# Weight parts by turns in one tile: a projection kernel whose stationary reads step by 8 bytes

## The chip, the cores and the metric

The kernel runs on one core of one Trainium2 chip. The metric is the device time of one execution in microseconds. The time of the kernel before is the median of three runs; a profiled execution of the same program is read beside them.

## What is computed

One decoder layer on x of 512 tokens by 1024 channels, in float32. The input is RMS-normalised, projected by `w_in`, passed through four token mixers, gated, merged and projected once more:

```python
h = rmsnorm(x, norm_pre)
u = h @ w_in                                   # 1024 x D_IN, D_IN holds all projections
branches = (gdn(u), gla(u), ssd(u), nsa(u))    # four mixers of 512 channels each
gates = sigmoid(u['merge_gate'])               # 4 x 1024 channels
merged = sum(gates[n] * (branches[n] @ w_br[n]) for n in range(4))
x = x + rmsnorm(merged @ w_out, norm_post)
```

Most of the arithmetic is `h @ w_in`: 84 blocks of 1024 by 128 (or 512 by 256) weights.

## The kernel before, in words

Matrix products are done in float32r, a float32 type that TensorE takes in one pass and in which it keeps fewer bits. So that no precision is lost, each operand is split into a high part (rounded to float32r) and a low part (what the rounding left), and each product is three matmuls: high by high, high by low and low by high (`mm3`, L759). The normalised input is held all the time in `hhi` and `hlo`, tiles of 128 partitions by 8 blocks by 512 tokens (L678, L679).

A block of weights is fetched by SyncE's queue into a staging tile `ws`, 128 by 1024 float32. ScalarE copies it to `wh` (the high part), VectorE subtracts that from `ws` and writes `wl` (the low part). This is `wload` (L735 to L757). `ws` has three buffers, `wh` and `wl` two each (L611). The first two loads have their low part made by GpSimd (L752).

Three kinds of products use these weights:

- `proj_ft` (L765) gives 128 channels by 512 tokens. Weights are the stationary operand: 8 slices of 128 columns of `wh` and of `wl`, loaded 24 times for 24 matmuls of 512 columns over `hhi` and `hlo`. Such a matmul is written `big<-hhi,wh` in the profile: output, moving operand, stationary operand. The first two calls run in halves of 256 columns and in another order.
- `proj_tf` and the output projection (L781) give 128 tokens by 256 channels. There the weights are the moving operand, in slices of 256 columns, and `hhi` or `hlo` is the stationary one (`tf<-wh,hhi`).
- The branch projections in `merge` (L1689) use weights from `w_br` as the stationary operand, with the split branch output `yh`, `yl` moving (`big<-yh,wh`).

One more group, at L808 to L822, puts 56 narrow columns into a `wh` tile and multiplies with 120 and 56 stationary columns.

The order of instructions is not the order of the code. `Sched` (L303) records every operation with the buffers it touches, prices it, and places all of them by a list scheduler on a model of the five engines; `emit` (L477) then issues them in that order. Dependencies in that plan come from `View.mask` (L131), which marks a tile in groups of 8 elements. Tags in `S.fifo` (L613) are handed out in the order of the load groups. Tiles without a tag live in one pool and get their address when they are first issued; those in `S.first` (L682) come ahead of all others. The waits on the chip are worked out from the operations as issued.

In all traces every instruction carries line L519, that of the helper which records it; so groups are told apart by tile names.

Of the kernel before, what the change touches and what calls it, by code (L numbers as in the profile page):

```python
# [7 lines left out]
F32 = mybir.dt.float32  # L8
BF16 = mybir.dt.bfloat16
F32R = mybir.dt.float32r  # L10
# [5 lines left out]
P = 128  # L16
# [3 lines left out]
ND = D // P  # L20
# [17 lines left out]
def f32(ap):  # L38
    return ap.bitcast(F32)


NG = 34
N4 = 12
# [555 lines left out]
def block_kernel(ctx, tc, a, out):  # L599
    nc = tc.nc  # L600
    W = a['w_in'][0]
# [6 lines left out]
    psum = mkpool("psum", space=PSUM)  # L608
    dram = mkpool("dram", space=bass.MemoryType.DRAM)
    pools = {None: (const, 1), 'big': (psum, 3), 'sm': (psum, 5)}  # L610
    for tag, n in (('g', NG), ('t4', N4), ('ws', 3), ('wh', 2), ('wl', 2), ('cv', 3), ('k1', 10), ('tiny', 12)):  # L611
        pools[tag] = (work, n)
    S = Sched(tc, pools, ('ws', 'wh', 'wl', 'cv', 'big'))  # L613
    act, dve, pool, pe, sp = (Engine(S, e, r) for e, r in (('ACT', nc.scalar), ('DVE', nc.vector), ('POOL', nc.gpsimd),
                                                            ('PE', nc.tensor), ('SP', nc.sync)))
    after = S.order

    def big(name="big"):
        return S.buf(name, [P, T], F32, 'big', 'psum')

    def sm(name="sm"):
        return S.buf(name, [P, T], F32, 'sm', 'psum')

    def w2(name, cap=None, dt=F32):
        return S.buf(name, [P, T], dt, 'g')

# [3 lines left out]
    def t4(name, dt=F32, shape=(P, 2, T)):  # L630
        return S.buf(name, shape, dt, 't4')

# [12 lines left out]
    def cst(name, shape, dt=F32):  # L645
        return S.buf(name, shape, dt, None)
# [30 lines left out]
    loads = []  # L677
    hhi = cst("hhi", [P, ND, T], F32R)  # L678
    hlo = cst("hlo", [P, ND, T], F32R)  # L679

    al12 = cst("al12", [P, 12], F32)
    S.first += [al12, hhi, hlo]  # L682
    xts = []
    for tt in range(NT):
        xt = t4("xt", shape=(P, D))
# [38 lines left out]
    pe.transpose(pt[:, :P], rows, ident)  # L724
    act.copy(cols, pt[:, :P])

    dtb12 = cst("dtb12", [P, 12], F32)
    for dst, na, ncc in ((al12, 'a_log_a', 'a_log_c'), (dtb12, 'dt_bias_a', 'dt_bias_c')):
        for nm, o, n in ((na, 0, 4), (ncc, 4, 8)):
            src = a[nm]  # L730
# [1 line left out]
    dskip = bcast_row('d_skip_c', 8)  # L732


    def wload(srcs, cut, shape, res=(), group=True):  # L735

        if group:
            S.grp += 1
        st, hi, lo = (S.buf(nm, [P, 1024], dt, nm).rearrange(cut, **shape)
                      for nm, dt in (('ws', F32), ('wh', F32R), ('wl', F32R)))  # L740
        o = 0
        for i, src in enumerate(srcs):
            n = src.shape[-1]
            op = sp.dma_start(st[:, :, o:o + n], src)
            if i == 0:
                op.resv = [v.buf for v in res]
            loads.append(op)
            o += n
        early = len(loads) <= 2
        S.urgent = 0 if early else -1  # L750
        c = act.copy(hi, st)
        t = (pool if early else dve).tensor_sub(lo, st, f32(hi))  # L752
        S.urgent = None
        if early:

            c.key, t.key = (0, xload.prio[1] + 40), (0, xload.prio[1] + 41)
        return hi, lo, op  # L757

    def mm3(ps, sh, sl, mh, ml, first, last, shared=False):  # L759
        i = pe.matmul(ps, sh, mh, start=first, stop=False, skip_group_check=shared)  # L760
        pe.matmul(ps, sh, ml, start=False, stop=False, skip_group_check=shared)
        pe.matmul(ps, sl, mh, start=False, stop=last, skip_group_check=shared)
        return i

    def proj_ft(c0, *res, group=True):  # L765
        hi, lo, _ = wload([W[:, c0:c0 + P].rearrange("(a p) f -> p a f", p=P)], "p (a f) -> p a f", dict(f=P), res, group)
        ps = big()
        if len(loads) > 2:
            for d in range(ND):
                mm3(ps, hi[:, d], lo[:, d], hhi[:, d], hlo[:, d], d == 0, d == ND - 1)  # L770
            return ps

        for o in (0, T // 2):
            t = slice(o, o + T // 2)
            pairs = [(hi, hhi, d) for d in range(ND)] + [(hi, hlo, d) for d in range(ND)] + [(lo, hhi, d) for d in range(ND)]
            for i, (w, m, d) in enumerate(pairs):
                pe.matmul(ps[:, t], w[:, d], m[:, d, t], start=i == 0 and o == 0, stop=i == len(pairs) - 1,
                          skip_group_check=True)
        return ps
# [15 lines left out]
    def tf_load(srcs, kh, res=(), group=False):  # L795
        hi, lo, _ = wload([src[kh * 512:(kh + 1) * 512].rearrange("(a p) f -> p a f", p=P) for src in srcs],
                          "p (a f) -> p a f", dict(f=256), res, group)
        return hi, lo
# [9 lines left out]
    S.grp += 1  # L808
    late = []
    LO = 64  # L810
    st, hi = (S.buf(nm, [P, 1024], dt, nm).rearrange("p (a f) -> p a f", f=P) for nm, dt in (('ws', F32), ('wh', F32R)))
    for nm, o, n in (('gla_gk', 0, 16), ('gdn_beta', 16, 8), ('ssd_dt', 24, 8), ('nsa_gate', 32, 24)):
        src = W[:, OFF[nm]:OFF[nm] + n].rearrange("(a p) f -> p a f", p=P)
        late.append(sp.dma_start(st[:, :, o:o + n], src))
# [114 lines left out]
    def zproj_ft(name):  # L929
        z = Feat("z")  # L930
        for c in range(4):
            ps = proj_ft(OFF[name] + c * P, z[c])
            silu2(z[c], ps)
        return z
# [54 lines left out]
    def gdn():  # L989
        qkv = [None] * 12  # L990
        for c in (4, 5, 6, 7, 0, 1, 2, 3, 8, 9, 10, 11):
            if c < GPAIR:
                if c % 2 == 0:
                    pair = t4("gqk")
                t = pair[:, c % 2]
            else:
                t = w2("gqkv")
            ps = proj_ft(OFF['gdn_q'] + c * P, t)
            conv_silu(t, ps, R_CA, 12, c, None)
            qkv[c] = t  # L1000
            n = sum(v is not None for v in qkv)
            if n <= 2:
                loads[-1].key = (0, xload.prio[1] + 0.1 * n)
            elif n == 4:
                for i, op in enumerate(late):
                    op.key = (1, len(S.ops) - 1 + 0.1 * (i + 1))
# [199 lines left out]
    def ssd():  # L1206
        xbc = []
        for c in range(8):
            t = w2("gqkv")
            ps = proj_ft(OFF['ssd_x'] + c * P, t)  # L1210
            conv_silu(t, ps, R_CC, 8, c, cols[:, R_CB + c:R_CB + c + 1])
            xbc.append(t)
# [476 lines left out]
    def merge(n):  # L1689
# [5 lines left out]
        for d2 in range(ND // 2):  # L1695
            ds = (2 * d2, 2 * d2 + 1)
            first = merged[ds[0]] is None
            if first:
                for d in ds:
                    merged[d] = w2("merged")  # L1700
            ths = []
            for i, d in enumerate(ds):
                psg = proj_ft(OFF['merge_gate'] + n * D + d * P, *([merged[v] for v in ds] if first and i == 0 else []),
                              group=i == 0)
                if i == 0:
                    for e in ready:
                        S.order(loads[-1], e)
                th = S.buf("mth", [P, T], F32, 'cv')
                act.activation(th, psg, AF.Tanh, scale=0.5)
                ths.append(th)  # L1710
            src = a['w_br'][0, n][:, d2 * 256:(d2 + 1) * 256].rearrange("(b p) f -> p b f", p=P)
            hi, lo, _ = wload([src], "p (b f) -> p b f", dict(f=256), group=False)
            for i, d in enumerate(ds):
                th = ths[i]
                ps = big()
                for b in range(4):
                    fs = slice(i * P, (i + 1) * P)
                    mm3(ps, hi[:, b, fs], lo[:, b, fs], yh[b], yl[b], b == 0, b == 3)
                if first:
                    dve.scalar_tensor_tensor(merged[d], th, 1.0, ps, op0=OP.add, op1=OP.mult)  # L1720
                else:
                    dve.scalar_tensor_tensor(th, th, 1.0, ps, op0=OP.add, op1=OP.mult)
                    m_ops.append(pool.tensor_add(merged[d], merged[d], th))
# [17 lines left out]
    for q in range(4):  # L1741
# [9 lines left out]
        else:  # L1751
# [3 lines left out]
            for tt in range(NT):  # L1755
                for d in range(ND):
                    s = slice(tt * P, (tt + 1) * P)
                    hi, lo = parts[d // 4]
# [49 lines left out]
```

## Time and profile before

| | us |
|---|---|
| median of 3 runs | 824.61 (823.39 to 826.69) |
| profiled execution, its own time | 824.95 |
| span in the profile, first to last instruction | 823.2 |
| TensorE matmul busy | 798.4 (97%) |
| TensorE weight loads busy | 678.2 (82%) |
| VectorE busy | 500.3 (61%) |
| ScalarE busy | 373.8 (45%) |
| GpSimd busy | 206.6 (25%) |

The busy time of matmuls overlaps itself, since one starts before the one ahead of it has drained: the length of a matmul in a row says less than the distance from its start to the start of the next. Weight loads are recorded apart (PEld); the load for a matmul runs beside the matmul ahead of it. The mean granted TensorE clock is 0.995 of full speed.

### The profile page before, as it was taken

To read this page: it belongs to the slowest core of one execution; us is meant where nothing else is said; L and a number is where in the kernel's file an instruction comes from. 1 tells how busy PE (TensorE), PEld (TensorE's weight loads), DVE (VectorE), ACT (ScalarE), POOL (GpSimd) and SP (SyncE) were. 2 spreads that over 40 slices of the span, in tenths; PEclk is the share of its full clock that TensorE was granted. 3 is DMA by queue.
4 is the path that set the end of the run, shared out by engine and by line. 5 is a ranking of instruction groups with operands and counts; after the bars stand their busy time and mean duration, and the time that the engine had idled before them with its cause. 6 is when DMAs were issued, how large, how long until landed. Compare 5 with 4: busy or idle time off the path is not lost.

```text
span 823.2 us, 12822 instructions
## 1 busy us (share of the span) xinstructions
PE 798.4 (97%) x4772; PEld 678.2 (82%) x4772; DVE 500.3 (61%) x1112; ACT 373.8 (45%) x878; POOL 206.6 (25%) x254
## 2 busy tenths in 40 slices
PE   5999999999999999999999899998999999999996
PEld 5888888887888899888887677897888888888996
DVE  5687766577545767777775977748533333343535
ACT  5344734323335767677654734644432222223432
POOL 6000273340131322222213400205521411121101
PEclk9999999999999999999999999999999999999998
DMA  7434254510132122211223231433133333334332
GB/s 229 93 105 128 77 136 105 129 27 2 52 103 76 52 53 52 77 52 53 68 61 77 52 77 52 115 104 103 52 97 85 101 102 103 87 94 127 115 143 103
DMA packets 112742, 72.39 MB, mean 88 GB/s; under 512 B 11788, under 2 KB 108232, under 8 KB 112680
## 3 DMA queue, kind: packets, MB, share of 16 engines
q1 hardware_dynamic: 111976, 69.86, 30.6%
q0 software_dynamic: 704, 1.70, 0.9%
q8 instruction: 38, 0.62, 0.3%
q14 instruction: 24, 0.20, 0.1%
HBM read 68.12 MB, written 3.43 MB: 87 GB/s over the span
## 4 chain that ended last, share of the span: by engine, by line
PE 89%; DVE 4%; ACT 2%; issue 2%; POOL 1%; DMA 1%; POOLq 0%; SPq 0%; DVEq 0%; ACTq 0%
PE big L519 58%; PE tf L519 12%; PE p_nsa L519 9%; PE p_gdn L519 5%; PE p_gla L519 2%; PE p_ssd L519 2%; DMA xt<-in_x 1%; DVE wl L519 1%; PE p_head_tail L519 1%; DVE gb L519 0%; POOL se L519 0%; ACT sq L519 0%; ACT wh L519 0%; PE p_h L519 0%; DVE cv L519 0%
## 5 line engine op out<-in xcount | busy, mean ns | idle before, releaser
L519 DVE TENSOR_TENSOR wl<-ws,wh 128x1024 fp32r<-128x1024 f32 x108 | 149.3, 1382 | 157.5 <-ACT wh L519 156.2
L519 PE MATMUL big<-hhi,wh 128*128 128x512 f32 (+2 forms) x632 | 242.4, 391 | 0.0
L519 PE MATMUL big<-hlo,wh 128*128 128x512 f32 (+1 forms) x632 | 241.3, 389 | 0.0
L519 PE MATMUL big<-hhi,wl 128*128 128x512 f32 (+1 forms) x624 | 237.3, 388 | 0.0
L519 ACT CAST wh<-ws 128x1024 fp32r<-128x1024 f32 (+1 forms) x111 | 116.1, 1047 | 243.0 <-PE big L519 199.3
L519 PEld LDWEIGHTS big<-hhi,wh 128*128 128x128 f32 (+1 forms) x632 | 118.1, 191 | 22.7 <-issue 0.5
L519 PEld LDWEIGHTS big<-hlo,wh 128*128 128x128 f32 x632 | 116.7, 188 | 22.8 <-issue 0.6
L519 PEld LDWEIGHTS big<-hhi,wl 128*128 128x128 f32 x624 | 115.7, 189 | 22.0 <-issue 0.8
L519 PE MATMUL tf<-wl,hhi 128*128 128x256 f32 x288 | 81.9, 285 | 0.0
L519 PE MATMUL tf<-wh,hhi 128*128 128x256 f32 x288 | 81.9, 285 | 0.0
L519 PE MATMUL tf<-wh,hlo 128*128 128x256 f32 x288 | 81.8, 285 | 0.0
L519 POOL TENSOR_SCALAR se<-se,r,ngate 128x128 f32<-128x128 f32 (+1 forms) x64 | 41.4, 649 | 152.8 <-DVE r L519 120.6
L519 POOL TENSOR_TENSOR merged<-merged,mth 128x512 f32<-128x512 f32 x24 | 33.1, 1379 | 143.8 <-DVE mth L519 143.8
L519 PEld LDWEIGHTS tf<-wh,hhi 128*128 128x128 f32 x288 | 55.0, 191 | 0.5
L519 PEld LDWEIGHTS tf<-wl,hhi 128*128 128x128 f32 x288 | 55.1, 192 | 0.4
L519 PEld LDWEIGHTS tf<-wh,hlo 128*128 128x128 f32 x288 | 55.1, 191 | 0.4
L519 PE MATMUL big<-yl,wh 128*128 128x512 f32 x128 | 50.3, 393 | 0.0
L519 PE MATMUL big<-yh,wh 128*128 128x512 f32 x128 | 50.1, 392 | 0.0
L519 PE MATMUL big<-yh,wl 128*128 128x512 f32 x128 | 50.1, 392 | 0.0
L519 ACT ACTIVATE se<-se,mn 128x128 f32<-128x128 f32 (+1 forms) x64 | 36.0, 563 | 24.1 <-DVE mn L519 22.8
L519 DVE SCALAR_TENSOR_TENSOR cv<-big,cols,cv 128x511 f32<-128x511 f32 (+2 forms) x60 | 44.5, 743 | 1.4 <-ACT cv L519 0.5
L519 DVE CUSTOM_DVE_ANT_0 se<-p_nsa,nb 128x128 f32<-128x128 f32 (+1 forms) x64 | 30.9, 482 | 8.1 <-PE p_nsa L519 7.7
(335 smaller groups left out, 1241.7 us busy)
## 6 DMA issues: line engine op xcount, KB each, us to landing
ws<-in_w_in SPq DMA_DIRECT2D x84, 512.0 KB, 3.9
ws<-in_w_br SPq DMA_DIRECT2D x16, 512.0 KB, 3.5
ws<-in_w_out SPq DMA_DIRECT2D x8, 512.0 KB, 3.4
rows<-scrG SPq DMA_DIRECT2D x12, 256.0 KB, 4.7
xt<-in_x SPq DMA_DIRECT2D x4, 512.0 KB, 3.5
xr<-in_x SPq DMA_DIRECT2D x4, 512.0 KB, 4.5
out<-xo SPq DMA_DIRECT2D x8, 256.0 KB, 2.6
scrA<-B POOLq DMA_DIRECT2D x4, 256.0 KB, 3.1
```

Of the source, the lines that this page charges most:

```text
L519: return fn(*[res(v) for v in args], **{k: res(v) for k, v in kw.items()})
```

## The change

`wh` and `wl` become one tile of 2048 float32r and 32 more that nothing uses (8320 bytes for each partition), with two buffers under one tag `w`. Since 8320 is 32 times 256 and 128 more, the second buffer begins at another remainder modulo 256 than the first. A new helper `wtile` gives the two halves. With `turns` the high and low part of each weight stand next to each other, so that a slice of 128 columns of either part spans 1024 bytes in steps of 8; without it the high parts fill the first 4096 bytes and the low parts the next. Only `proj_ft` asks for `turns`, and only from its third load on. The branch projections, the token-major projections and the narrow group use the tile without it. `dtb12`, 48 bytes, is allocated right behind `hlo` instead of later.

```diff
-    for tag, n in (('g', NG), ('t4', N4), ('ws', 3), ('wh', 2), ('wl', 2), ('cv', 3), ('k1', 10), ('tiny', 12)):
+    for tag, n in (('g', NG), ('t4', N4), ('ws', 3), ('w', 2), ('cv', 3), ('k1', 10), ('tiny', 12)):
...
-    S = Sched(tc, pools, ('ws', 'wh', 'wl', 'cv', 'big'))
+    S = Sched(tc, pools, ('ws', 'w', 'cv', 'big'))
...
-    S.first += [al12, hhi, hlo]
+    dtb12 = cst("dtb12", [P, 12], F32)
+    S.first += [al12, hhi, hlo, dtb12]
...
+    def wtile(a, f, turns):
+
+        t = S.buf("wp", [P, 2048 + 32], F32R, 'w')[:, :2048]
+        if turns:
+            t = t.rearrange("p (a f h) -> p a f h", a=a, h=2)
+            return t[:, :, :, 0], t[:, :, :, 1]
+        t = t.rearrange("p (h a f) -> p h a f", h=2, a=a)
+        return t[:, 0], t[:, 1]
+
-    def wload(srcs, cut, shape, res=(), group=True):
+    def wload(srcs, cut, shape, res=(), group=True, turns=False):
...
-        st, hi, lo = (S.buf(nm, [P, 1024], dt, nm).rearrange(cut, **shape)
-                      for nm, dt in (('ws', F32), ('wh', F32R), ('wl', F32R)))
+        f = shape['f']
+        st = S.buf('ws', [P, 1024], F32, 'ws').rearrange(cut, **shape)
+        hi, lo = wtile(1024 // f, f, turns)
...
-        hi, lo, _ = wload([W[:, c0:c0 + P].rearrange("(a p) f -> p a f", p=P)], "p (a f) -> p a f", dict(f=P), res, group)
+        hi, lo, _ = wload([W[:, c0:c0 + P].rearrange("(a p) f -> p a f", p=P)], "p (a f) -> p a f", dict(f=P), res, group,
+                          turns=len(loads) >= 2)
...
-    st, hi = (S.buf(nm, [P, 1024], dt, nm).rearrange("p (a f) -> p a f", f=P) for nm, dt in (('ws', F32), ('wh', F32R)))
+    st = S.buf('ws', [P, 1024], F32, 'ws').rearrange("p (a f) -> p a f", f=P)
+    hi = wtile(ND, P, False)[0]
```

## Rows read from the trace of the kernel before

**Rows 1.** The page, part 1 (busy time by engine) and part 4 (chain by engine).
```profile
PE 798.4 (97%) x4772; PEld 678.2 (82%) x4772; DVE 500.3 (61%) x1112; ACT 373.8 (45%) x878; POOL 206.6 (25%) x254
PE 89%; DVE 4%; ACT 2%; issue 2%; POOL 1%; DMA 1%; POOLq 0%; SPq 0%; DVEq 0%; ACTq 0%
```

**Rows 2.** Groups by form: line, engine, operation, out<-in, shapes, count | busy, mean ns.
```profile
L519 PE MATMUL big<-hhi,wh 128*128 128x512 f32 x592 | 234.1, 395 | 0.0
L519 PE MATMUL big<-hlo,wh 128*128 128x512 f32 x592 | 233.8, 395 | 0.0
L519 PE MATMUL big<-hhi,wl 128*128 128x512 f32 x592 | 232.9, 394 | 0.0
```

**Rows 3.** Timeline of PE matmuls, 661 to 667 us: start us, length us, instruction.
```profile
661.28 0.39 PE L519 MATMUL big<-hhi,wl 128*128 128x512 f32 x1
661.50 0.39 PE L519 MATMUL big<-hhi,wh 128*128 128x512 f32 x1
...
666.72 0.39 PE L519 MATMUL big<-hhi,wl 128*128 128x512 f32 x1
```

**Rows 4.** Timeline of PE matmuls, 545 to 546 us, weights moving, 256 columns.
```profile
544.92 0.28 PE L519 MATMUL tf<-wh,hlo 128*128 128x256 f32 x1
...
545.88 0.28 PE L519 MATMUL tf<-wl,hhi 128*128 128x256 f32 x1
```

**Rows 5.** Groups by form, weight loads of 128, 120, 56 and 64 columns.
```profile
L519 PEld LDWEIGHTS big<-hhi,wh 128*128 128x128 f32 x624 | 116.7, 191 | 22.0 <-issue 0.5 <-DVE gat L519 0.3
L519 PEld LDWEIGHTS big<-hhi,wh 128*120 128x120 f32 x8 | 1.4, 181 | 0.7
L519 PEld LDWEIGHTS big<-hlo,wh 128*56 128x56 f32 x8 | 1.0, 128 | 0.4
L519 PEld LDWEIGHTS p_gdn<-XX,Ao 64*64 64x64 f32 x128 | 5.1, 134 | 2.0 <-issue 0.8
L519 PEld LDWEIGHTS p_nsa<-kcv,cw 128*64 128x64 f32 x64 | 6.7, 151 | 0.1
```

**Rows 6.** Timeline of PEld, 557 us: loads beside float32 matmuls of 256 columns.
```profile
556.99 0.19 PEld L519 LDWEIGHTS p_ssd<-xdd,cb 128*128 128x128 f32 x1
557.21 0.19 PEld L519 LDWEIGHTS p_ssd<-xdd,cb 128*128 128x128 f32 x1
557.42 0.19 PEld L519 LDWEIGHTS big<-hlo,wh 128*128 128x128 f32 x1
```

**Rows 7.** Timeline of PE matmuls, 408 to 410 us, behind a change of operands.
```profile
408.57 0.40 PE L519 MATMUL big<-hhi,wl 128*128 128x512 f32 x1
408.81 0.40 PE L519 MATMUL big<-hhi,wh 128*128 128x512 f32 x1
409.05 0.39 PE L519 MATMUL big<-hlo,wh 128*128 128x512 f32 x1
409.28 0.39 PE L519 MATMUL big<-hhi,wl 128*128 128x512 f32 x1
```

**Rows 8.** Timeline of PE matmuls, 35 to 37 us: the narrow group.
```profile
35.51 0.40 PE L519 MATMUL big<-hlo,wh 128*56 128x512 f32 x1
...
36.90 0.40 PE L519 MATMUL big<-hlo,wh 128*56 128x512 f32 x1
```

**Rows 9.** Loads of transposes by form, and the matmul before one, 262 us.
```profile
L519 PEld LDWEIGHTS p_nsa<-ident,se 128*128 128x128 f32 x160 | 19.9, 140 | 7.6 <-POOL se L519 3.6
...
261.86 0.39 PE L519 MATMUL big<-hhi,wl 128*128 128x512 f32 x1
262.09 0.38 PE L519 MATMUL p_nsa<-ident,se 128*128 128x128 f32 x2
```

**Rows 10.** Timeline of PE matmuls, 177 us: moving operand in steps of 64 bytes.
```profile
177.17 2.76 PE L519 MATMUL p_nsa<-kcv,cw 128*64 128x62 f32 x24
```

**Rows 11.** Timelines of ACT, DVE and PEld: one load's conversion and its first use.
```profile
666.91 1.05 ACT L519 CAST wh<-ws 128x1024 fp32r<-128x1024 f32 x1 [3.90 <-PE big L519]
668.00 1.23 DVE L519 TENSOR_TENSOR wl<-ws,wh 128x1024 fp32r<-128x1024 f32 x1 [4.22 <-ACT wh L519]
672.16 0.19 PEld L519 LDWEIGHTS big<-hhi,wh 128*128 128x128 f32 x1
```

**Rows 12.** The same for a load whose subtraction is slow.
```profile
657.12 2.34 DVE L519 TENSOR_TENSOR wl<-ws,wh 128x1024 fp32r<-128x1024 f32 x1
661.28 0.19 PEld L519 LDWEIGHTS big<-hhi,wh 128*128 128x128 f32 x1
```

**Rows 13.** Stretch 250 to 500 us: busy time of all engines; then matmuls on `hlo` alone.
```profile
250.00:500.00 250.00, 245.27 (x1411) 205.04 (x1409) 180.59 (x574) 160.40 (x410) 64.94 (x91) 0.99 0.23 62
250.00:500.00 250.00, 84.23 (x231) 43.72 (x230) 0.00 (x0) 0.99 0.23 62
```

More of the change, by code (lines that the diff above doesn't have):

```diff
@@ L725, in block_kernel @@
     act.copy(cols, pt[:, :P])
-    dtb12 = cst("dtb12", [P, 12], F32)
     for dst, na, ncc in ((al12, 'a_log_a', 'a_log_c'), (dtb12, 'dt_bias_a', 'dt_bias_c')):
```

## The prediction

> **What bounds the kernel now.** I read the page's busy times and its chain first: TensorE is busy for 97% of the span and holds 89% of the chain that ended last [rows 1]. So a change matters if it alters how fast TensorE goes through its instructions, or makes it wait. Next I read the groups by form, to see how many instructions the change touches: 592 matmuls for each of the three products of `proj_ft`, 1776 in all, each with a load of 128 stationary columns that will step by 8 bytes [rows 2]. Then the timeline of TensorE in the merge stages, for the distance between starts: from 661.28 to 666.72 us there are 24 matmuls, 5.44 us, so 226.7 ns each [rows 3]. The matmuls of 256 columns come 8 in 0.96 us, 120 ns each [rows 4]. The difference, 106.7 ns for 256 columns, is 0.417 ns a column, the upper of the two clock levels (2.4 GHz; the granted clock is 0.995). By that 512 columns are 213.3 ns, and in both forms 13.3 ns are left over for each matmul. This remainder is what the change can touch: 1776 times 13.3 ns is 23.6 us.
>
> **What the remainder may be.** A load of 120 columns takes 181 ns and one of 56 takes 128 [rows 5], so 0.83 ns for each further column, half the pace of the moving columns. So one instruction reads `hhi` or `hlo` at 4 bytes in 0.417 ns while the other reads weights at 4 bytes in 0.83 ns, from the same memory. Three rows bear on whether the two hinder each other. For: beside float32 matmuls, which take their columns at half the pace, three loads of 128 columns start within 0.43 us, so some 216 ns apart (the rows end at 10 ns), while 256 columns pass; at half the pace these are 213.3 ns, so only about 2.7 ns are left beside a load of the same size [rows 6]. For: behind a change of operands the same matmul is slower and settles only after some repeats: from 408.57 to 409.28 us three of them take 0.71 us, 237 ns each, against 226.7 in the steady run [rows 7, 3]. A fixed price for taking up new weights would not change from one repeat to the next; two readers that meet in time would. Against: in the narrow group the loads have 120 and 56 columns by turns, a third fewer bytes, and six matmuls take 1.39 us, 232 ns each [rows 8].
>
> **The change part by part.**
>
> *The 8-byte step.* The stationary read then moves through memory at 8 bytes in 0.83 ns, which is the pace of the moving read, 4 bytes in 0.417 ns. Today the faster reader passes over the places of the slower one again and again; at equal pace the two keep their distance, so that after one delay they need not meet again. Lower end: what is left is the 2.7 ns of the float32 rows [rows 6], 216 ns a matmul, a saving of 10.7 ns. Upper end: the 10.7 ns go with the bytes that a load spans, which double, so 10.7 ns more. The nearest row to reading at equal pace is the load of a transpose: 140 ns where one of the same 128 columns otherwise takes 191 [rows 9, 5]; the 51 ns between them are about half of 128 times 0.83, so it reads at about double pace. The matmul beside it takes from 261.86 to 262.09 us, 0.23, and so shows no saving; but it stands at a change of operands, where [rows 7] are slow as well, and all work tiles there begin at one remainder modulo 256 (their sizes added up in the order of allocation give 192 for `hhi`, `hlo`, `wh`, `wl` and the tiles of the attention). After the change the second buffer begins 128 bytes off. I take the lower end, since the float32 rows and the settling both speak for meeting readers, and give it a chance to match that doubt.
>
> The sum: 1776 times 10.7 ns is 18.9 us. In the stretch from 250 to 500 us lie 231 of the 592 matmuls on `hlo` [rows 13], so 693 of the 1776 and 7.4 us of the saving. There they fill gaps between attention steps that wait for VectorE, ScalarE and GpSimd. VectorE is busy for 181 of 250 us there [rows 13], so it is not full, but a filler that ends earlier uncovers some waits: I give back a third, 2.5 us (ends: nothing, and all 7.4). That makes 16.4 us. The profiled execution took 824.95 us, 1.75 more than its span, and lies 0.34 above the median; 824.95 less 16.4 is 808.5.
>
> *The longer reach of a load.* If stepping slowed the load itself, nothing would show at first: without a step 128 columns at 0.83 ns are 107 ns of reading, and there are 216 to hide in. The only strided read by TensorE is `kcv`, in steps of 64 bytes: 24 matmuls of 62 columns in 2.76 us, about 108 ns each when the tail of 0.28 is taken off, 1.7 ns a column, which is double the 0.84 ns of the float32 rows [rows 10, 6]; the load beside it goes from 134 to 151 ns [rows 5]. Doubled, a load of 128 columns would be 213 ns and still just fit. I take nothing.
>
> *Writing by turns.* ScalarE's copy and VectorE's subtraction now write, and VectorE reads, in steps of 8 bytes. No row shows such a step on these engines. Lower end: no change. Upper end, from the pace of [rows 10] against [rows 6]: double. The cover is in the merge stages' timeline: copy at 666.91, 1.05 us, subtraction at 668.00, 1.23 us, ready at 669.23, first used at 672.16, a reserve of 2.93 us [rows 11]. Doubling both takes 2.3. Where the subtraction takes 2.34 us, since GpSimd adds to `merged` meanwhile, the reserve is 1.82 us [rows 12], and lengthened by the same 2.3 the ten such loads in the merge stages would be 0.5 us late each, 5 us. Faster matmuls cut the reserve by 24 times 10.7 ns, 0.26 us. I take nothing.
>
> *One tile for two.* The copy for the next load now waits until the last matmul on the low part is done as well: one matmul, 0.23 us, out of the 2.93. If waits are worked out for a span of bytes and not for each element, the first load of a group waits for VectorE's subtraction where it waited for ScalarE's copy; it starts 2.93 us after that [rows 11]. The plan also sees high and low parts in the same groups of 8 elements, so it may order some instructions otherwise; I put that at 2 us either way and take nothing.
>
> *The rest.* The loads of the branch projections, the token-major ones and the first two are as they were. `dtb12` moves `ident` by 64 bytes. Transposes read it; if each of some 300 gained or lost a remainder of 13.3 ns it would be 4 us either way; nothing taken. SyncE's DMAs are the same in number and size.
>
> **A rule against the change.** The row: beside loads of any width, 512-column matmuls keep at least 13.3 ns, even in the narrow group [rows 3, 8]. The Trainium skill, "TensorE: Matmul & The Clock Gate", Part 2, step ①, says that the engine has two independent read ports, and that loading the next weights takes no read bandwidth from the running matmul. By that rule the sum would be 0 and the time 825. The trace agrees in the narrow group and disagrees in [rows 6 and 7]. A second rule, in "SBUF — State Buffer", Door 1, says that SBUF has 16-byte lines, that an access to a new line costs extra and that two hits in a line suffice for full bandwidth. It would make the sum zero or worse: an 8-byte step has those two hits but crosses 64 lines for 32. No row here shows lines.
>
> **The rivals.**
>
> *One buffer gains, the other stays.* The two buffers lie differently to `hhi` and `hlo`. If only one distance avoids the meeting, half of the loads save: 9.4 us less a third of 39%, 8.2; 816.5. Chance 0.17.
>
> *The remainder is a fixed price of a float32r matmul.* Then the step does nothing. For it: [rows 4 and 3] leave the same 13.3 ns at 256 and 512 columns, and [rows 8] show no gain from shorter loads. Against: [rows 6 and 7]. 825, from 822 to 828 by the plan's order. Chance 0.25.
>
> *The stall goes with the bytes that a load spans.* Place: the same 1776 matmuls; price: the 10.7 ns that float32 rows do not have doubles. TensorE is the bound, so all of it shows: 824.95 and 18.9 are 844; with one buffer alone, 834. It decides as soon as the mean distance of starts in a steady run goes over 226.7 ns. For it: the load of a transpose, which reads at equal pace, leaves its neighbour at 230 and not lower [rows 9]. Chance 0.28.
>
> **How the numbers follow.** Forecast 808.5 us, chance 0.30; its own range is 804 to 813 (nothing given back, and all of it). With the one-buffer case faster by over 0.5% has 0.47, and a little from the plan's order makes 0.48; within 0.5% (about what a measurement of this kernel can tell from no change) 0.24; slower 0.28. The range that should hold 8 in 10 goes from 804 (nothing given back, 806, and 2 us from the plan's order) over the unchanged case to 835 (the loss on one buffer, 834, rounded up); left out is the loss on both, about 0.18.
>
> **What the profile after would show.** Right: in a run of 24 matmuls of the merge stages the distance falls from 226.7 to about 216 ns, while `big<-yh,wh`, which isn't turned, stays at 226.7. Some new waits between 250 and 500 us for attention's softmax chain. Copy and subtraction at 1.05 and 1.23 us. One buffer alone: loads alternate between two distances. Fixed price: 226.7 stays. Loss: above 226.7. The prediction is wrong at its root if the distance doesn't fall, and in its size if it falls but attention gives back more.

## The result and the profile after

The changed kernel takes 836.24 us (835.31 to 836.78, four runs) where the kernel before, run on the same chip, takes 825.01: a ratio of 1.0135, 95% interval 1.0112 to 1.0158. The forecast of 808.5 has the wrong sign, and the time lies above the range.

The page after, its busy times, its chain by engine and the groups that answer to [rows 1, 2 and 5]:

```profile
PE 806.9 (97%) x4772; PEld 689.4 (83%) x4772; DVE 497.7 (60%) x1112; ACT 378.6 (45%) x878; POOL 204.6 (25%) x254
...
PE 86%; DVE 5%; ACT 4%; issue 2%; POOL 2%; DMA 1%; POOLq 0%; SPq 0%; DVEq 0%; ACTq 0%
...
L519 PE MATMUL big<-hhi,wp 128*128 128x512 f32 (+1 forms) x1256 | 396.1, 392 | 0.9 <-DVE wp L519 0.9
L519 PEld LDWEIGHTS big<-hhi,wp 128*128 128x128 f32 x1256 | 238.4, 195 | 44.6 <-issue 2.1
L519 DVE TENSOR_TENSOR wp<-ws,wp 128x1024 fp32r<-128x1024 f32 (+1 forms) x109 | 146.6, 1345 | 167.7 <-ACT wp L519 167.4
L519 ACT CAST wp<-ws 128x1024 fp32r<-128x1024 f32 (+1 forms) x111 | 121.6, 1096 | 249.3 <-PE big L519 198.6
```

TensorE is still the bound, at a granted clock of 0.996; the busy time of matmuls rose by 8.5 us. The mean length of a matmul tells little (392 against 395 ns), so the distance between starts must be read. In the timeline of TensorE in a merge stage four loads follow each other; of each, the first and the last of the matmuls on the low part of the data stand here (`hlo` or `yl`, every third matmul):

```profile
659.46 0.40 PE L519 MATMUL big<-yl,wp 128*128 128x512 f32 x1
...
664.24 0.39 PE L519 MATMUL big<-yl,wp 128*128 128x512 f32 x1
...
664.93 0.40 PE L519 MATMUL big<-hlo,wp 128*128 128x512 f32 x1
...
669.79 0.40 PE L519 MATMUL big<-hlo,wp 128*128 128x512 f32 x1
...
670.48 0.39 PE L519 MATMUL big<-hlo,wp 128*128 128x512 f32 x1
...
675.38 0.39 PE L519 MATMUL big<-hlo,wp 128*128 128x512 f32 x1
...
676.08 0.39 PE L519 MATMUL big<-yl,wp 128*128 128x512 f32 x1
...
680.96 0.39 PE L519 MATMUL big<-yl,wp 128*128 128x512 f32 x1
```

Each pair spans 21 matmuls. They take 4.78, 4.86, 4.90 and 4.88 us, so 227.6, 231.4, 233.3 and 232.4 ns each, where 226.7 stood [rows 3]. Buffers are used by turns: the first and the third run read from the first buffer, which begins at the same remainder modulo 256 as `hhi`, the second and the fourth from the second, 128 bytes further. So the turned loads are slower on either buffer, and a load of the branch projections, which isn't turned, is slower on the second buffer alone. (Below, "the distance" of a buffer is this offset modulo 256; times from start to start are named as such.)

The waits of TensorE's weight loads after (columns: engine, line, waited for; us in total, times, longest):

```profile
PEld p_nsa L519 <- POOL se L519: 5.4, 10, 1.0
PEld p_nsa L519 <- DVE cl L519: 2.8, 6, 0.6
PEld big L519 <- DVE wp L519: 1.3, 1, 1.3
```

and the same rows before:

```profile
PEld p_nsa L519 <- POOL se L519: 3.6, 8, 1.1
PEld p_nsa L519 <- DVE cl L519: 1.7, 5, 0.5
```

So TensorE also waits more in attention. To divide the loss, I add up the intervals from each matmul's start to the next start over the whole trace. In us, for before, for the joint tile alone, for the joint tile with the distance, and for the whole change (the two between are experiments below):

| intervals | before | joint tile | and distance | after |
|---|---|---|---|---|
| `proj_ft`, 512 columns, up to 245 ns | 379.1 | 378.4 | 383.5 | 388.4 |
| the same, 245 to 500 ns | 32.0 | 33.7 | 33.0 | 29.9 |
| branch projections, up to 500 ns | 88.2 | 88.5 | 89.7 | 89.7 |
| any, over 500 ns (waits) | 17.4 (18) | 21.0 (23) | 19.9 (22) | 21.9 (24) |
| all | 808.8 | 813.5 | 818.4 | 819.5 |

From before to after that is 10.7 us, of 11.0 in the spans: 7.2 in `proj_ft`, 1.5 in the branch projections, 4.5 in waits, less 2.5 elsewhere. The joint tile alone already has 1.0 of the 7.2 and 3.6 of the 4.5.

### The profile page after: what moved, and what is told of

The parts are those of the page before. It is cut to its first block, busy times and chain, and to the rows that moved or that the text cites. A ratio compares the mean times of both kernels' runs of the same rounds, so it can differ in the third digit from the quotient of the medians.

```text
span 834.2 us, 12794 instructions
## 1 busy us (share of the span) xinstructions
PE 806.9 (97%) x4772; PEld 689.4 (83%) x4772; DVE 497.7 (60%) x1112; ACT 378.6 (45%) x878; POOL 204.6 (25%) x254
## 4 chain that ended last, share of the span: by engine, by line
PE 86%; DVE 5%; ACT 4%; issue 2%; POOL 2%; DMA 1%; POOLq 0%; SPq 0%; DVEq 0%; ACTq 0%
PE big L519 57%; PE tf L519 11%; PE p_nsa L519 8%; PE p_gdn L519 5%; PE p_gla L519 2%; PE p_ssd L519 2%; DVE wp L519 1%; ACT wp L519 1%; DMA xt<-in_x 1%; DVE cl L519 1%; POOL se L519 1%; ACT ch L519 1%; PE p_head_tail L519 1%; DMA rows<-scrG 1%; DVE gb L519 0%
## 5 line engine op out<-in xcount | busy, mean ns | idle before, releaser
L519 PE MATMUL big<-hhi,wp 128*128 128x512 f32 (+1 forms) x1256 | 396.1, 392 | 0.9 <-DVE wp L519 0.9
L519 PEld LDWEIGHTS big<-hhi,wp 128*128 128x128 f32 x1256 | 238.4, 195 | 44.6 <-issue 2.1
L519 DVE TENSOR_TENSOR wp<-ws,wp 128x1024 fp32r<-128x1024 f32 (+1 forms) x109 | 146.6, 1345 | 167.7 <-ACT wp L519 167.4
L519 PE MATMUL big<-hlo,wp 128*128 128x512 f32 (+1 forms) x632 | 243.4, 393 | 0.0
L519 ACT CAST wp<-ws 128x1024 fp32r<-128x1024 f32 (+1 forms) x111 | 121.6, 1096 | 249.3 <-PE big L519 198.6
L519 PEld LDWEIGHTS big<-hlo,wp 128*128 128x128 f32 x632 | 120.8, 194 | 20.4
L519 PE MATMUL tf<-wp,hhi 128*128 128x256 f32 x576 | 107.5, 284 | 0.0
L519 PEld LDWEIGHTS tf<-wp,hhi 128*128 128x128 f32 x576 | 90.3, 190 | 1.0
L519 PE MATMUL big<-yh,wp 128*128 128x512 f32 x256 | 83.8, 395 | 0.0
L519 PE MATMUL tf<-wp,hlo 128*128 128x256 f32 x288 | 81.5, 284 | 0.0
```

Of the source, the lines that this page charges most:

```text
L519: return fn(*[res(v) for v in args], **{k: res(v) for k, v in kw.items()})
```

## The experiments

The first question was which of the three parts costs: the step of 8 bytes, the distance of the second buffer, or one tile for two.

**The joint tile alone.** No turns, no spare bytes:

```diff
-        t = S.buf("wp", [P, 2048 + 32], F32R, 'w')[:, :2048]
+        t = S.buf("wp", [P, 2048], F32R, 'w')[:, :2048]
-                          turns=len(loads) >= 2)
+                          turns=False)
```

> Neither turns nor spare columns: only one tile for two under one tag, with the place of dtb12 as changed. Theories D and S: 825, distance of starts 226.7 in steady runs everywhere. Theory T: 836.

830.05 us, ratio 1.0057 (1.004 to 1.0074), between what D and S said and what T said. The 512-column matmuls start 227.8 ns apart on average (intervals up to 245 ns), as before. So something costs 4.7 us that is not the pace of TensorE in steady runs; the table shows 3.6 of it as waits. I come back to it.

**The distance, without turns.** The change with `turns=False` alone:

> The changed kernel with the turns undone: high parts in the first half of the tile, low parts in the second, so every load of stationary columns steps by 4 bytes again; the second buffer stays 128 bytes off modulo 256. Theory D (the time of a matmul hangs on the distance modulo 256 between the weights' slice and the moving tile, and on the step): loads of the buffer 128 bytes off leave their neighbour at about 232 ns as the branch projections' do in the changed kernel, those of the other at 226.7; half of the 1776 and half of the 384 at 5 ns more are 5.4 us, so 830. Theory S (only the step costs): 825. Theory T (one tile for two, its waits and the plan's new order cost): 836.

834.58 us, ratio 1.0109 (1.0094 to 1.0124), so 4.5 us more than the joint tile alone. Theory D's 5.4 us is near that; its 830 had nothing for the tile. Timeline of TensorE, matmuls on the low part of the data, a run on either buffer:

```profile
664.37 0.40 PE L519 MATMUL big<-hlo,wp 128*128 128x512 f32 x1
...
669.25 0.40 PE L519 MATMUL big<-hlo,wp 128*128 128x512 f32 x1
669.95 0.40 PE L519 MATMUL big<-hlo,wp 128*128 128x512 f32 x1
...
674.72 0.39 PE L519 MATMUL big<-hlo,wp 128*128 128x512 f32 x1
```

4.88 us for 21 is 232.4 ns on the second buffer, 4.77 is 227.1 on the first. No read steps by 8 bytes here.

**Turns, without the distance.** The change with a tile of `[P, 2048]`:

> The changed kernel with the 32 spare columns left out: both buffers begin at the remainder of the moving tiles. Theory D: all turned loads leave their neighbour at 233 to 234 ns, as those of that buffer do in the changed kernel, branch projections go back to 226.7; 1776 times 6.8 ns is 12.1 us, so 837. Theory S: the same as the changed kernel within 1 us but for the branch projections, 835 to 836. Theory T: 836. If the pad was what cost: 825.

838.13 us, ratio 1.0157 (1.0139 to 1.0176), 8.1 us above the joint tile alone. Theory D's 837 came near by luck: it had 12.1 us for the step and nothing for the tile. Both buffers are the same now:

```profile
665.10 0.39 PE L519 MATMUL big<-hlo,wp 128*128 128x512 f32 x1
...
670.00 0.39 PE L519 MATMUL big<-hlo,wp 128*128 128x512 f32 x1
670.70 0.39 PE L519 MATMUL big<-hlo,wp 128*128 128x512 f32 x1
...
675.60 0.39 PE L519 MATMUL big<-hlo,wp 128*128 128x512 f32 x1
676.30 0.39 PE L519 MATMUL big<-yl,wp 128*128 128x512 f32 x1
...
681.06 0.39 PE L519 MATMUL big<-yl,wp 128*128 128x512 f32 x1
```

4.90 us for 21 turned ones is 233.3 ns, 4.76 for the branch projection 226.7. So the step costs 6.6 ns where the distance is 0, and with turns the spare bytes gain a little (231.4 against 233.3 on the second buffer) where without turns they lose. That is why turns cost 8.1 us here and only 1.7 on top of the distance. By the pace alone it would be more: 1776 times 6.6 ns is 11.7 us. Part is taken back where the matmuls fill gaps between the mixers' steps: the load that starts at 460.5 us in the joint tile starts 4.5 us later with turns, the one at 512.2 only 2.5 us later.

**The distance alone.** To be sure that the distance needs no joint tile: the kernel before with its own tiles and order, and 128 spare bytes for each.

```diff
-        st, hi, lo = (S.buf(nm, [P, 1024], dt, nm).rearrange(cut, **shape)
-                      for nm, dt in (('ws', F32), ('wh', F32R), ('wl', F32R)))
+        st, hi, lo = (S.buf(nm, [P, n], dt, nm)[:, :1024].rearrange(cut, **shape)
+                      for nm, n, dt in (('ws', 1024, F32), ('wh', 1024 + 32, F32R), ('wl', 1024 + 32, F32R)))
...
```

(The tiles of the narrow group get the same spare bytes.)

> The kernel before with separate tiles for the high and the low part, no turns, its own order; only 128 spare bytes behind each of the wh and wl tiles, so that both second buffers begin 128 bytes further modulo 256. Distance theory (the pad by itself slows every load from the second buffer by some 4 to 5 ns, whatever the tile is): 888 of the 1776 proj_ft matmuls at 232 to 233 ns where 227.5 stood, 4.3 us, and half of the branch projections a little: 829 to 831 us, ratio 1.005 to 1.007, first buffer still at 227 to 228. Rival (the slower second buffer needs the joint tile or the changed order): 825 us, ratio within 0.002 of 1, both buffers at 227 to 228.

829.14 us, ratio 1.0057 (1.004 to 1.0074). The distance theory holds; the rival, 825 us, falls. In the timeline:

```profile
661.20 0.40 PE L519 MATMUL big<-hlo,wh 128*128 128x512 f32 x1
...
665.97 0.39 PE L519 MATMUL big<-hlo,wh 128*128 128x512 f32 x1
666.67 0.40 PE L519 MATMUL big<-hlo,wh 128*128 128x512 f32 x1
...
671.55 0.40 PE L519 MATMUL big<-hlo,wh 128*128 128x512 f32 x1
```

4.77 us, 227.1 ns each, and then 4.88, 232.4. Over the trace the mean is 228.4 beside the first buffers and 232.7 beside the second. In this run and in all others only the weights were moved; `hhi` and `hlo` stayed where they were. So the runs show that the pace hangs on where the weights lie modulo 256. That it is their distance to the moving tile, and not their place by itself, is not shown.

**A scan of distances.** Is there a distance at which a step of 4 or of 8 bytes gains? The joint tile, with its start 16 bytes further for every second load:

```diff
-        t = S.buf("wp", [P, 2048 + 32], F32R, 'w')[:, :2048]
+        off = 4 * (len(wtiles) // 2 % 16)
+        wtiles.append(off)
+        t = S.buf("wp", [P, 2048 + 64], F32R, 'w')[:, off:off + 2048]
```

once with `turns=False`:

> A measurement: high and low parts in halves (step of 4 bytes), and each pair of loads begins 16 bytes further into its tile than the pair before, from 0 to 240, round and round, both buffers alike. Theory D: the distance of starts of 512-column matmuls is a function of this offset, 226.7 at 0 and 232 at 128, with other values between; at some offset it may fall below 226.7. Theory S or T: 226.7 at every offset.

and once with turns:

> A measurement: the turned layout with the offset of each pair of loads within its tile moving on by 16 bytes, 0 to 240, both buffers alike. If equal pace of the two readers helped at some distance (the step of the prediction that is in doubt), some offset shows starts well under 226.7 ns, down to 216; if the step only ever adds, every offset lies between 229 and 236.

One run each: 838.4 and 834.98 us. The addresses follow from the sizes in the order of allocation; joined to the starts in the trace they give the mean time from start to start of 512-column matmuls in ns (70 to 121 intervals for each figure with a step of 4, 25 to 75, on the high parts, with 8), by how far the weights lie from the moving tile modulo 256:

```
bytes      0    16    32    48    64    80    96   112   128   144   160   176   192   208   224   240
step 4 228.3 229.5 233.2 233.3 233.2 232.1 234.2 233.2 233.4 233.5 233.3 229.9 229.0 233.3 233.4 227.3
step 8 233.1 232.7 232.3 231.0 230.0 232.1 231.2 230.0 231.2 233.1 233.9 233.3 233.6 231.5 233.3 231.4
```

Reading at equal pace helps at no distance: the best is 230.0. With a step of 4 bytes there is a floor near 227 and a plateau near 233, and 0, where the kernel before has all of its tiles, lies on the floor. So neither scan points to a version that is better than before, and none was run.

**Does the remainder depend on the load at all?** The kernel before, with 64 of 128 stationary columns from the second channel block on (half of the sum over these blocks is left out):

```diff
-                mm3(ps, hi[:, d], lo[:, d], hhi[:, d], hlo[:, d], d == 0, d == ND - 1)
+                if d == 0:
+                    mm3(ps, hi[:, d], lo[:, d], hhi[:, d], hlo[:, d], True, False, True)
+                else:
+                    mm3(ps[:64], hi[:, d, :64], lo[:, d, :64], hhi[:, d], hlo[:, d], False, d == ND - 1, True)
```

> The kernel before, but in proj_ft from the third load on only the first block of the contraction uses 128 stationary columns; the seven others load 64, so that half of the output channels leave out seven eighths of their sum. Same instructions in the same order, half the bytes for 21 of 24 loads. If the remainder of 13.3 ns goes with the bytes of a load: starts 220 ns apart in steady runs, 10 us less in all. If it is a fixed price of a float32r matmul: 226.7 and 825. If it hangs on how the two readers meet: something else than either, possibly different from repeat to repeat.

826.3 us in one run; over its trace a matmul with 64 columns beside its own kind starts 229.9 ns before the next (mean of 1332 intervals up to 245 ns), where the kernel before has 227.6. Then the same with 128, 96, 64 or 32 columns, by turns of the loads:

> The kernel before; each proj_ft load uses 128, 96, 64 or 32 of its 128 stationary columns by turns from its second channel block on, so the rest of those channels' sums is left out. Fixed price (the 13.3 ns above 512 columns at full clock belong to each float32r matmul and not to the load beside it): 226.7 to 230 ns from start to start at every width. Rival (the remainder goes with the bytes that a load reads): 226.7, 223.3, 220 and 216.7 ns for 128, 96, 64 and 32 columns. The time is 822 to 828 us by the first and about 815 us by the second.

826.85 us in one run. The groups of loads by form (busy us, mean ns):

```profile
L519 PEld LDWEIGHTS big<-hhi,wh 128*96 128x96 f32 x126 | 20.4, 162 | 7.2
L519 PEld LDWEIGHTS big<-hhi,wh 128*32 128x32 f32 x133 | 14.5, 109 | 13.4
```

and from the timeline of TensorE three runs, of 128, 96 and 32 columns, the first and last matmul on the low part of the weights of each:

```profile
657.38 0.39 PE L519 MATMUL big<-hhi,wl 128*128 128x512 f32 x1
...
662.82 0.39 PE L519 MATMUL big<-hhi,wl 128*128 128x512 f32 x1
663.51 0.39 PE L519 MATMUL big<-hhi,wl 128*96 128x512 f32 x1
...
667.65 0.40 PE L519 MATMUL big<-hhi,wl 128*96 128x512 f32 x1
...
674.48 0.39 PE L519 MATMUL big<-hhi,wl 128*32 128x512 f32 x1
...
678.64 0.40 PE L519 MATMUL big<-hhi,wl 128*32 128x512 f32 x1
```

5.44 us for 24 is 226.7 ns; 4.14 and 4.16 for 18 are 230.0 and 231.1. The load shrinks to 109 ns, and the matmul beside it gains nothing; it even loses 3 to 4 ns. The rival by bytes had 216.7 for 32 columns. Over the whole trace the means are 228.3, 230.1, 230.3 and 231.7 ns for 128, 96, 64 and 32 columns (intervals up to 245 ns). So the 13.3 ns don't go with the bytes that are read beside a matmul. Whether they belong to the float32r matmul or are a price of taking up a load of any size is not separated: each of the 4772 matmuls has a load of its own. The float32 rows, with 2.7 ns left beside loads of 128 columns [rows 6], speak against the second.

**What the joint tile costs.** It is 4.7 us in its own order. To see what the new order does, the same kernel in the order of before:

```diff
...
-        order = self.schedule()
+        order = [self.ops[int(i)] for i in ORDER_BEFORE.split()]
...
```

> The run with one tile only (no turns, no spare columns), but every engine's instructions in the order of the kernel before, written into the kernel as a list. Theory O (the 4.4 us of that run come from the plan's new order, which leaves attention waiting): 825 to 826, waits as before. Rival W (they come from the waits on the chip that one tile for two brings): 830.

833.74 us, ratio 1.0102 (1.0075 to 1.013). Theory O falls, and rival W's 830 was too low: in the order of before the tile costs 8.4 us (6.2 to 10.7 by the interval), and its new order takes back some 3.7. The trace shows how. ScalarE and TensorE at one place in attention, here (the recording helper is at L685 in this kernel, at L520 in the two with an extra copy below):

```profile
345.22 0.39 PE L685 MATMUL big<-hlo,wp 128*128 128x512 f32 x1
...
346.22 0.68 PE L685 MATMUL big<-hhi,wp 128*128 128x512 f32 x2
...
349.13 0.39 PE L685 MATMUL p_nsa<-ph,Vs 128*128 128x256 f32 x1 [0.86 <-ACT ph L685]
...
346.70 1.05 ACT L685 CAST wp<-ws 128x1024 fp32r<-128x1024 f32 x1 [1.48 <-PE big L685]
```

and before:

```profile
343.44 0.39 PE L519 MATMUL big<-hlo,wh 128*128 128x512 f32 x1
...
344.43 0.45 PE L519 MATMUL big<-hhi,wl 128*128 128x512 f32 x1
...
346.34 0.33 PE L519 MATMUL p_nsa<-ph,Vs 128*128 128x256 f32 x1
...
343.86 1.05 ACT L519 CAST wh<-ws 128x1024 fp32r<-128x1024 f32 x1 [0.42 <-PE big L519]
```

Before, the cast starts as soon as the last matmul on the old high part has ended (343.44 and 0.39 are 343.83). In the joint tile it starts behind the last one on the low part (346.22, the first of two), which is 1.00 us further down TensorE's queue, because seven matmuls of attention lie between. The cast waits 1.48 us where it waited 0.42; attention's copy `ph` stands behind it in ScalarE's queue, and TensorE is held 0.86 us for `ph` at 349.13. The weight loads' waits for `ph` over the trace, here

```profile
PEld p_nsa L685 <- ACT ph L685: 6.4, 9, 1.3
```

and before:

```profile
PEld p_nsa L519 <- ACT ph L519: 1.1, 5, 0.3
```

So 6.4 us for 1.1. This holds for the order of before. In the order as planned, the run with the joint tile alone has other waits:

```profile
PEld p_nsa L519 <- POOL se L519: 5.9, 12, 1.1
PEld p_nsa L519 <- DVE cl L519: 2.9, 6, 0.6
PEld p_nsa L519 <- ACT ph L519: 0.6, 3, 0.3
```

The wait for `ph` is shorter there than before; what grew are the waits for `se` and `cl`, by 3.5 us. How much of the 4.7 us as planned is still the release, and how much the plan's order by itself, no run separates.

The whole change in the order of before:

> The changed kernel (turns, spare columns) in the order of the kernel before. Theory O with D: only the distance of starts differs from before; 888 loads at 231.5 and 888 at 233.4 instead of 226.7 to 227.5 and half of the branch projections at 232 are some 9 to 10 us, so 834 to 835. Rival W: 836 to 839 as the waits of one tile, and of turned halves in it, come on top. Theory S alone (8 bytes cost the same at each distance): all turned loads leave their neighbour at one value.

841.96 us, ratio 1.02 (1.0185 to 1.0215): above rival W's 836 to 839, and 8.2 us on top of the run above, a little under the 9 to 10 that step and distance cost by the pace.

That the held cast is the cause was still read from rows alone. So the kernel before, with separate tiles, all addresses and the order unchanged, got the wait alone: ahead of each cast ScalarE copies one column into the load's `wl` tile. (`S.ahead` only sees to it that this tile has its address by then.)

```diff
...
-                for b in list(o.bufs) + o.resv:
+                for b in list(o.bufs) + o.resv + self.ahead.get(id(o), []):
...
         c = act.copy(hi, st)
+        S.ahead[id(c)] = [lo.buf] if 'lo' == 'lo' else []
+        first, whole = lo[:, :1, :1], c.fn
+
+        def both():
+            nc.scalar.copy(first.real(), st[:, :1, :1].real())
+            return whole()
+
+        c.fn = both
```

> The kernel before with its separate tiles and its own order; ahead of each cast into wh ScalarE copies one column of the block into the wl tile of the same load, so the cast stands in ScalarE's queue behind the last matmul on the old low part, as in a joint tile, while addresses, tiles and order of all other work stay. Theory (the joint tile costs by this release: ScalarE's in-order queue holds the attention's ph behind the cast): 8.8 us as in the joint tile with the old order, less at most 1 or 2 us if part of that was something else, on top of the twin run that copies the same column into wh; 831 to 835 us. Rival (the joint tile costs by something else, such as waits for VectorE's part): within 2 us of the twin.

Its twin copies the same column into `wh` (`first, whole = hi[:, :1, :1], c.fn`):

> The twin: the same extra copy of one column, into wh, which the cast had to wait for anyway. It prices the extra instruction: some 110 copies of one column on ScalarE, which is busy 45% of the span. 825 to 828 us by every theory; if short ScalarE work before a cast costs more than that by itself, the run with wl is read against this one.

836.28 us, ratio 1.0143 (1.0118 to 1.0168), and for the twin 829.21, 1.0064 (1.0049 to 1.0079). Both lie just over 1 us above their ranges. By the medians the wait costs 7.1 us beyond the twin, by the ratios 6.5, of the 8.4 to be explained. Timeline of ScalarE at the same place, with the wait:

```profile
346.82 0.19 ACT L757 CAST wl<-ws 128x1 fp32r<-128x1 f32 x1 [1.48 <-PE big L520]
346.92 1.04 ACT L520 CAST wh<-ws 128x1024 fp32r<-128x1024 f32 x1
```

and its weight loads' waits:

```profile
PEld p_nsa L520 <- ACT ph L520: 7.1, 9, 1.4
```

Timeline and waits of the twin:

```profile
344.92 0.19 ACT L757 CAST wh<-ws 128x1 fp32r<-128x1 f32 x1 [0.43 <-PE big L520]
345.14 1.05 ACT L520 CAST wh<-ws 128x1024 fp32r<-128x1024 f32 x1
```

```profile
PEld p_nsa L520 <- ACT ph L520: 2.5, 8, 0.5
```

The same 1.48 us as in the joint tile, and nearly the same sum of waits. So in the order of before the release is the cause of most of the 8.4 us; the rest, under 2 us, lies within the intervals. The twin is not quite even: its casts start 0.22 us behind the start of the copy on average, those of the run with the wait 0.11, so it prices the extra copy too high rather than too low. The twin's own 4.95 us (829.21 less 824.26) were more than expected: 110 copies of one column, 0.19 us each, on an engine that is busy 45% of the time.

**`dtb12` alone**, moved ahead in the kernel before:

> The kernel before with only the move of dtb12 in front of the other work tiles. Every theory here: 825 us, ratio within 0.003 of 1. If the move of ident and its transposes were part of the joint tile's 4.4 us, it would be 827 to 829.

825.03 us, ratio 1.0006 (0.9996 to 1.0015): nothing.

## Why the prediction was wrong

- *What bounds it:* right. TensorE stays the bound, and a change of its pace shows: half of the 1776 matmuls at 5.3 ns more (232.4 for 227.1) are 4.7 us, and the run with the distance alone lost 4.4. It doesn't always show in full (8.1 of 11.7 us with turns alone), so the part that was given back in the prediction's sum has a counterpart.
- *The 8-byte step,* the term of 18.9 us: wrong in sign. Taken at 10.7 ns gained for each of 1776 matmuls; measured 6.6 ns lost at distance 0 (233.3 against 226.7) and 4.7 lost on the second buffer (231.4), where the distance alone had lost 5.7 (232.4). The step that failed is the choice of the lower end from [rows 6 and 7]. That the float32 matmuls leave only 2.7 ns does not carry over to float32r ones. Nor does the settling in [rows 7]: what the runs moved, by the weights' place and the step, is the part above some 227 ns, up to 234; nothing moved the floor of 13.3 ns. That two readers that meet make the upper part is not shown. [Rows 8 and 9] had pointed the other way (less to load or an equal pace, and no gain) and were the nearer rows, being 512-column float32r matmuls themselves; I explained them away.
- *The rule that loading takes no read bandwidth* (the Trainium skill, "TensorE: Matmul & The Clock Gate", Part 2, step ①): the trace agrees as far as amount goes, since a load of 32 columns costs its neighbour no less than one of 128. It disagrees as far as place goes: the same load moved by 128 bytes costs its neighbour 5 ns. By the rule the sum was 0; measured were 6.2 us lost in `proj_ft` against the joint tile, for step and distance together. The second rule (the Trainium skill, "SBUF — State Buffer", Door 1) had left zero or worse, and worse it was: at distance 0 a step that crosses twice as many 16-byte lines costs 6.6 ns a matmul. Whether lines are the cause no run here shows.
- *The distance of the second buffer* stood in the prediction only as a doubt about the gain. As a cost of its own, with the weights read as before, it was missing; the run with nothing else measures 4.4 us (829.14 less 824.69). The prediction had noticed that all tiles of before lie at one remainder, but not that this may be what keeps the matmuls at 226.7 ns.
- *One tile for two,* taken at nothing: measured 4.7 us as planned, 8.4 in the order of before. The failed step is the cover: "one matmul, 0.23 us, out of the 2.93" is right for the merge stages of [rows 11], and I used it for the whole kernel. Where attention's matmuls lie between a load's last ones the cast was held 1.06 us longer in the order of before, and `ph` waits behind it. Queued behind the waiting cast on ScalarE was what ought to have been listed. The plan's order, put at 2 us either way, gained some 3.7 on that and left 4.7, of which 3.5 show as longer waits for `se` and `cl`.
- *Waits for VectorE's subtraction,* the other half of that term: once in the whole trace, 1.3 us.
- *Longer reach of a load:* hidden, as said: 195 ns, against 190 in the kernel with the distance and no turns.
- *Writing by turns:* held. The cast goes from 1.05 us to about 1.1, the subtraction is as long as before.
- *The rest* (`dtb12`, SyncE's DMAs): held.
- *The sum.* [Rows 13] were misread. Of the 231 matmuls on `hlo` between 250 and 500 us, 167 are `big<-hlo,wh`; the other 64 are `tf<-wh,hlo`, where `hlo` is the stationary operand. So 501 of the 1776 lie there and not 693, and the forecast would have been some 0.7 us lower. The one-buffer rival's 824.95 less 8.2 is 816.75, not 816.5. Neither matters beside the wrong sign.
- *The rivals.* The fixed price was right that 13.3 ns stay, and wrong about the time. Of the rival by which the stall goes with the bytes spanned, the sign and the place came true, and its point of decision (a mean time from start to start over 226.7 ns) was the right one to look at. Its price did not: 13.3 ns do not go with bytes, and the doubling to 237 ns was not seen. That its 834 for one buffer lies near the measured 836.24 is luck: both buffers lost, and 4.7 us are the joint tile's. One buffer that gains: on the contrary, the second buffer loses even without turns.

## What to carry to other kernels

Before a fixed remainder of every instruction is put down to a conflict, shrink the suspected neighbour: had the prediction trusted the row in which narrower loads gave nothing back, the whole saving would have gone. Where tiles that are read together happen to begin at one remainder, that may already be the good case, so a change of sizes or paddings is priced with both signs. And when two buffers are joined, look at each stage for the last reader of the joined tile, and at what is queued behind the instruction that waits for it.

## What was not expected of the hardware

- A float32r matmul of 512 columns keeps a remainder of 13.3 ns above its 213.3 beside loads of any size (109 to 191 ns long), and up to 7 ns more by the place of the weights modulo 256 and the step, with the moving tiles left in place. What sets the good distances (0, 240, and less so 16, 176 and 192 at a step of 4) wasn't found out.
- Why float32 matmuls leave only 2.7 ns [rows 6] was not tried.
- The turned kernels have 3 us less in `proj_ft`'s intervals of 245 to 500 ns (29.9 for 33.0); this was not pursued.
